# A two-layer attention, scan and convolution block: the attention's value product turned round, exponentials stationary and values moving

## The chip, the core and the metric

The kernel runs on one core of one Trainium2 chip. The metric is the device time of one execution in microseconds (us). The core's engines each run their own queue of instructions in order: the tensor engine (PE in the profile, its weight loads PEld), the vector engine (DVE), the scalar engine (ACT), GpSimd (POOL) and SyncE (SP), which here issues all DMAs. PE multiplies a stationary operand, loaded first, with a moving one, and writes to PSUM; the others bring the result back to SBUF.

## The reference, cut to what matters

Two layers run over 1024 tokens and a prefix of 256 context tokens, with a width of 1024. In each layer one projection feeds three branches: a bidirectional state space scan (12 heads of 64), an attention with 12 query heads of 64 on 4 key and value heads, and a gated convolution. Their outputs are joined and go through an output projection. In the last layer only the 1024 tokens are carried on. The attention is

```python
s = jnp.einsum('bqkrd,bskd->bkrqs', qi, keys, preferred_element_type=F32) * scale
p = jax.nn.softmax(s, axis=-1).astype(vals.dtype)
return jnp.einsum('bkrqs,bskd->bqkrd', p, vals)
...
attn_lat = attend(ql, jnp.concatenate([kl, kc], axis=1), jnp.concatenate([vl, vc], axis=1)) * jax.nn.silu(ga)
```

All of it is in float32. The 1024 queries attend to all 1280 keys, the 256 context queries of the first layer to the 256 context keys alone.

## The kernel before, in words

A layer runs through an input projection (`phase_b`), the attention (`attn_prep`, `attn`) beside the scan (`ssd`), and the output projection (`wout_half`, `out_half`). Projections and scores split each float32 operand into a high and a low part of type F32R, and multiply the parts; the value product, the scan and the column of twos use plain F32.

The attention works on units: a pair of query heads `p` (6 of them) and a group `g` of 256 queries. Layer 0 has 5 groups, the last of them the context, and layer 1 has 4, so there are 30 and 24 units. A unit of ordinary queries goes over 10 key tiles of 128 keys, a context unit over 2. A unit has these parts:

- `prep` (`qprep`, `kprep`): query and key blocks are loaded, split and transposed on PE into the PSUM bank "v", of which there is one, and copied to `q_a`, `q_b`, `k_a`, `k_b`.
- `maxima`: scores with queries on the partitions (rows `m<-k_a,q_a`), whose row maxima DVE takes (`a_sm`, L924). They become a row beside the queries, so that the score matmul subtracts them.
- `scores`: for each key tile, scores with keys on the partitions and 2 x 256 queries along the free axis (rows `m<-q_a,k_a` and `m<-q_b,k_b`), and their exponentials `a_p` by ACT (128x512). DVE and POOL add the exponentials of pairs of key tiles up (L963, L967, L970), which leaves one 128x512 tile `a_a2` a unit.
- `values`: for each key tile two matmuls. The stationary operand is a value block of 128 keys x 64, the moving one the exponentials of one head, 128 keys x 256 queries. The two heads use the two 64-column halves of the array and fill partitions 0 to 63 and 64 to 127 of a bank of PSUM pool "t". The output is feature-major: 128 features of the head pair by 256 queries. A plain F32 matmul shows in the trace as two passes, each with its load.
- `finish`: two matmuls with a stationary block of twos on `a_a2` give twice the sum of the exponentials, spread over all features (rows `t<-a_a,twos`). DVE takes the reciprocal (L994) and multiplies (L995), POOL multiplies by the gate (L996), and a DMA stores the block into `ya_d`. The two stands for a half that the gate in `ga_d` lacks.

The loop at the end of `attn` interleaves the units. In each step of a key tile it calls the scores, the maxima of the unit two ahead, the values two steps behind (VLAG), and at step 7 the finish of a unit whose values are complete. Each call sets a priority (`at`); the framework simulates the engines and fixes the order of each engine's queue from these priorities and from what is ready in its simulation. The scan has priorities of its own in the same stretch of time, and its matmuls (rows `x<-...`) stand in the same PE queue. It uses many POOL operations; `s_e` with `s_xd` also uses the two halves of the array. The output weights are loaded into memory that the scan frees, those of the second half of the output into memory that the attention frees.

In the code below, `mk` takes a tile from a pool, `mm` is a matmul (out, stationary, moving, start, stop; L191), `tr` a transpose on PE (L194), `act` an activation (L197); V, G and Y are DVE, POOL and SP.

Of the kernel before, what the change touches and what calls it, by code (L numbers as in the profile page):

```python
# [11 lines left out]
ALU = mybir.AluOpType  # L12
# [10 lines left out]
SSD_PACE = 25.0  # L23
AT_PACE = 1.2
VLAG = 2
PTB = 5
AHEAD = 2
FLAG = 7
NG = [0, 1]
A2B = 1  # L30
GATP = True
GB = 2
DM = 1024
NLAT = 1024
# [124 lines left out]
def build(tc, a, out, depth=DEPTH, dump=None):  # L159
# [53 lines left out]
                mm(ps, xs(xi, k), ys(yi, k), first and i == 0, last and i == n - 1)  # L213
                i += 1

# [1 line left out]
    ccr = mk(cp, [128, KT, 2], "ccr")  # L217
    Y.dma_start(out=ccr, in_=a["cc"])
    msk = mk(cp, [128, 3, 128], "msk")
# [3 lines left out]
    V.tensor_copy(idr, idf)  # L223
    ones = mk(cp, [128, 128], "ones")
    G.memset(ones, 1.0)
    twos = mk(cp, [128, 64], "twos")
    G.memset(twos, 2.0)
    neg = mk(cp, [128, 16], "neg")
    G.memset(neg, -0.5)
    colc, rowc = [], []  # L230
# [15 lines left out]
    msh = [mk(cp, [128, KT, 2], f"msh{l}") for l in range(depth)]  # L246
    msc = [mk(cp, [128, KT, 2], f"msc{l}") for l in range(depth)]

# [1 line left out]
    x_d = [[dr([128, 512], f"x_d{t}_{n}") for n in range(2)] for t in range(NT)]  # L250
    q_d = [dr([NT, 128, 256], f"q_d{j}") for j in range(3)]
    k_d = dr([NT, 128, 256], "k_d")
# [15 lines left out]
        ts(V, tmp, i, scale, ALU.mult, EPS, ALU.add)  # L268
        G.tensor_tensor(o, tmp, neg[:, :n], ALU.pow)

# [1 line left out]
    def ada(l, j0, nj, lo, w, wp, bufs):  # L272
        ps = mk(pt, [128, 512], "t")
        for k in range(KT):
# [37 lines left out]
    def rc(l, n):  # L312
        return rowc[l][:, RO[n][0]:RO[n][0] + RO[n][1]]

# [1 line left out]
    def norm_tile(l, t, h, wp):  # L316
        r = 0 if t < 8 else 1
        xt = mk(wp, [128, DM], "n_x", bufs=3 if l == 0 else 1)
# [24 lines left out]
        V.tensor_copy(hh[:, :, tok], hf)  # L343
        (V if t % 2 else G).tensor_tensor(hl[:, :, tok], hf, hh[:, :, tok].bitcast(F32), ALU.subtract)

# [1 line left out]
    def wblock(p, rp, src, tag, bufs, e=None, rtag="wr", rbufs=1):  # L347
        shape = list(src.shape)
        hi = mk(p, shape, tag + "h", F32R, bufs=bufs)
# [18 lines left out]
        wk = wblock(wp, np_, a["wtm"][l, 0], "wk", 1, V, "n_h", 2 if l == 0 else 1)  # L368
        return st, h, ws, wk, ns, np_

    # ================= norm =================
    def norms(l, nh, b0, pace):
        for t in range(NT):
            at(b0 + t * pace)
            norm_tile(l, t, nh[1], nh[5])
        nh[4].close()

    # ================= SSD steps, decays and weights =================
    def ssd_prep(l, pp, tp):
        def sm(tag):  # L380
            return mk(pp if tag in ("d_dt", "d_cum", "d_ec", "d_et", "d_wd") else tp, [128, NT, 24], tag)
# [46 lines left out]
        Y.dma_start(out=cum_d.rearrange("(i r) t -> r i t", i=2), in_=ct)  # L428
        return dt, cum, ec, et, wd

    # ================= input projection =================
    def phase_b(l, nh, b0, pp):
        last = l == depth - 1
        st, st_r, s1 = ExitStack(), ExitStack(), ExitStack()
# [6 lines left out]
            norms(l, nh, b0 - 5, 2.6)  # L441
            nst.close()

# [1 line left out]
        qp = pool(s1, f"qp{l}")  # L445
        at(b0)
        rope = mk(qp, [128, 2, NT, 64], "rope")
# [81 lines left out]
                ada_gate(ll, ap_, 2)  # L529
        s1.close()  # L530

# [1 line left out]
        b2 = b0 + 130  # L533
        cmp_ = pool(st, f"cm{l}")
        s2 = ExitStack()
# [108 lines left out]
            block(i)  # L644
        s2.close()

# [1 line left out]
        s3 = ExitStack()  # L648
        tlp = pool(s3, f"tl{l}")
        g0 = b2 + 9 * 26  # L650
# [53 lines left out]
        st.close()  # L704
        return g0 + 8 * 26, sv, st_r

    # ================= SSD =================
    def ssd(l, sp, c0, sv):
        last = l == depth - 1
        at(c0)  # L710
# [123 lines left out]
                state(c, 0, xt, bt, hf, ho)  # L834
                hf = ho

    # ================= attention =================
    def attn_prep(l, kp, c0):
        last = l == depth - 1
        ng = 4 if last else 5  # L840
        at(c0 - 6)
        vs = mk(kp, [128, NT, 256], "vs")
        Y.dma_start(out=vs, in_=v_d.rearrange("t p f -> p t f"))
        kst = {}

        def kprep(v):
            ka = mk(kp, [128, NT, 128], "k_a", F32R, bufs=2)
            kb = mk(kp, [65, NT, 128], "k_b", F32R, bufs=2)
            act(kb[64:65], ones[64:65].unsqueeze(1).to_broadcast([1, NT, 128]), AF.Copy)
            for t0 in (0, 4, 8):  # L850
                n = min(4, NT - t0)
                kt = mk(kp, [128, 4, 64], "k_t", bufs=1)[:, 0:n]
                Y.dma_start(out=kt, in_=k_d[t0:t0 + n, :, 64 * v:64 * v + 64].rearrange("t p f -> p t f"))
                h2 = mk(kp, [128, 4, 2, 64], "k_h", F32R, bufs=1)[:, 0:n]
                l1 = mk(kp, [128, 4, 64], "k_l", F32R, bufs=1)[:, 0:n]
                act(h2, kt.unsqueeze(2).to_broadcast([128, n, 2, 64]), AF.Copy)
                V.tensor_tensor(l1, kt, h2[:, :, 0].bitcast(F32), ALU.subtract)
                ps = mk(pv_, [128, 4, 128], "v", F32R)
                for t in range(n):
                    tr(ps[:, t, :], h2[:, t].rearrange("p a d -> p (a d)"), idr)  # L860
                act(ka[:, t0:t0 + n, :], ps[:, 0:n, :], AF.Copy)
                ps = mk(pv_, [128, 4, 128], "v", F32R)
                for t in range(n):
                    tr(ps[0:64, t, :], l1[:, t], idr)
                act(kb[0:64, t0:t0 + n, :], ps[0:64, 0:n, :], AF.Copy)
            kst[v] = ka, kb

        def qprep(p, g):
            qt = mk(kp, [128, 2, 128], "q_t", bufs=2)
            Y.dma_start(out=qt, in_=q_d[p // 2][2 * g:2 * g + 2, :, 128 * (p % 2):128 * (p % 2) + 128].rearrange("t p f -> p t f"))  # L870
            sg = mk(kp, [128, 2, 2, 2, 64], "q_g", F32R, bufs=2)
            qv = qt.rearrange("p t (x d) -> p x t d", x=2)
            act(sg[:, :, :, 0, :], qv, AF.Copy)
            V.tensor_tensor(sg[:, :, :, 1, :], qv, sg[:, :, :, 0, :].bitcast(F32), ALU.subtract)
            ps = mk(pv_, [128, 2, 2, 128], "v", F32R)
            for x in range(2):
                for t in range(2):
                    tr(ps[:, x, t, :], sg[:, x, t].rearrange("p a d -> p (a d)"), idr)
            qa = mk(kp, [128, 2, 2, 128], "q_a", F32R, bufs=AHEAD + 2)
            qb = mk(kp, [65, 2, 2, 128], "q_b", F32R, bufs=AHEAD + 2)  # L880
            act(qa, ps, AF.Copy)
            act(qb[0:64], ps[0:64], AF.Copy)
            return qa, qb

        qst = {}
        units = [(p, g) for p in range(6) for g in range(ng)]

        def prep(i, t0):
            if i < len(units):
                p, g = units[i]  # L890
                at(t0)
                for v in sorted({(2 * p + y) // 3 for y in range(2)}):
                    if v not in kst:
                        kprep(v)
                qst[i] = qprep(p, g)

        for i in range(AHEAD + 1):
            prep(i, c0 - 5)
        return vs, kst, qst, prep, units

    def attn(l, ap, c0, pre):
# [3 lines left out]
        def key_tiles(i):  # L905
            return range(NT) if units[i][1] < 4 else range(8, NT)
# [1 line left out]
        def kv(i, x):  # L908
            return (2 * units[i][0] + x) // 3

        # row maxima of the scores, as a row beside the queries
        def maxima(i):
            qa, qb = qst[i]
            pcs = [(0, 512), (512, 512), (1024, 256)] if units[i][1] < 4 else [(1024, 256)]
# [15 lines left out]
            act(qb[64:65], ps[64:65].rearrange("p (x t) q -> p x t q", x=2), AF.Copy)  # L930
            yield

        pts, acs = {}, {}

        # exponentials of the scores by key tile, and their sums over the key tiles
        def scores(i):
            qa, qb = qst.pop(i)
            pts[i] = {}
            kt = key_tiles(i)
            ng = NG[i % len(NG)] if len(kt) > 2 else 0  # L940
            ac = [mk(ap, [128, 2, 512], f"a_ac{x}") for x in range(2)] if len(kt) > 2 else None
            prev = []
            same = kv(i, 0) == kv(i, 1)
            for b in kt:
                ps = mk(pm, [128, 512], "m")
                for x in range(1 if same else 2):
                    ka, kb = kst[kv(i, x)]
# [2 lines left out]
                    rb = qb.rearrange("p x t q -> p (x t q)") if same else qb[:, x].rearrange("p t q -> p (t q)")  # L950
                    mm(o, ka[:, b, :], ra, True, False)
                    mm(o, kb[:, b, :], rb, False, True)
                if b % 2 == 0:
                    pt2 = mk(ap, [128, 2, 512], "a_p", bufs=PTB)
                act(pt2[:, b % 2], ps, AF.Exp)
                pts[i][b] = pt2[:, b % 2]
                if b % 2:
                    j = b // 2
                    if not prev or j == ng + 1:
                        prev.append(pt2)  # L960
                    else:
                        e, o = (G, ac[0]) if j <= ng else (V, ac[1])
                        e.tensor_tensor(o, prev[-1], pt2, ALU.add)  # L963
                        prev[-1] = o
                yield
            if len(prev) > 1:
                V.tensor_tensor(ac[1], prev[0], prev[1], ALU.add)  # L967
                prev = [ac[1]]
            a2 = mk(ap, [128, 512], "a_a2", bufs=A2B)
            V.tensor_tensor(a2, prev[0][:, 0], prev[0][:, 1], ALU.add)  # L970
            acs[i] = a2
            yield

        def values(i):
            p, g = units[i]
            kt = key_tiles(i)
            gat = mk(ap, [128, 256], "a_g", bufs=GB)
            Y.dma_start(out=gat, in_=ga_d[p][:, 256 * g:256 * g + 256])  # L978
            ps = mk(pt, [128, 2, 256], "t")
            for b in kt:  # L980
                for y in range(2):
                    mm(ps[64 * y:64 * y + 64, 0, :], vs[:, b, 64 * kv(i, y):64 * kv(i, y) + 64],
                       pts[i][b][:, 256 * y:256 * y + 256], b == kt[0], b == NT - 1)
                yield
            pts.pop(i)
            fin.append((i, ps, gat))

        def finish(i, ps, gat):
            p, g = units[i]
            a2 = acs.pop(i)  # L990
            for y in range(2):
                mm(ps[64 * y:64 * y + 64, 1, :], twos[:, 0:64], a2[:, 256 * y:256 * y + 256], True, True)
            rc_ = mk(ap, [128, 256], "a_rc", bufs=1)
            V.reciprocal(rc_, ps[:, 1])  # L994
            V.tensor_tensor(rc_, ps[:, 0], rc_, ALU.mult)  # L995
            (G if GATP else V).tensor_tensor(gat, gat, rc_, ALU.mult)  # L996
            Y.dma_start(out=ya_d[p][:, 256 * g:256 * g + 256], in_=gat)

        t0 = c0
        for i in range(AHEAD):  # L1000
# [38 lines left out]
            finish(*fin.pop(0))  # L1039
        return t0  # L1040

    # ================= output projection =================
    def wout_half(l, n, wp, t0):
        w = []
        for k in [12, 13, 14, 15] + list(range(12)):
# [138 lines left out]
```

## Time and profile before

| | us |
|---|---|
| median of 3 runs | 2948.47 (2947.58 to 2953.2) |
| span of the profiled execution | 2948.2 |
| PE busy | 2799.6 (95%) |
| PE weight loads busy | 2059.6 (70%) |
| DVE busy | 2156.6 (73%) |
| ACT busy | 1066.1 (36%) |
| POOL busy | 1169.3 (40%) |
| attention, first to last exponentials, layer 0 | 826 to 1380 |
| attention, first to last exponentials, layer 1 | 2271 to 2757 |

A row of the timeline gives the start (us from the span's start), the length, the engine, the source line, the operation, the tiles it writes and reads, the shapes and how many neighbours were merged into it. `128*64` on a PE row are the rows and columns of the array in use. In brackets stands how long the engine was idle before it and what ended that; "issue" means that the profile shows nothing it waited for. A row of a stretch gives start:end and length, and then the busy time of PE, PEld, DVE, ACT and POOL with their instructions, the granted PE clock, the share of DMA and GB/s. A row of a group of instructions gives the count, then busy us and mean ns of one, then the idle time of the engine before them. A row of waits gives the waiting engine and line, what it waited for, total us, times and the longest.

### The profile page before, as it was taken

What the parts mean: (1) busy time and instruction counts of PE and PEld (TensorE: products, weight loads), DVE (VectorE), ACT (ScalarE), POOL (GpSimd) and SP (SyncE); (2) the same over time, 40 slices, a digit from 0 to 9 for tenths busy, and PEclk for the clock granted to TensorE, in tenths of its full rate; (3) what the DMA queues carried; (4) which work ended last, traced back from release to release, by engine and by line L of the source; (5) the groups of instructions that cost most, each with busy time, mean ns of one, the idle gap of its engine ahead of it and who ended that gap; (6) DMA issues with size and microseconds to landing.
All of it is one profiled execution on the core that took longest, in us unless ns stands there. A gap on an engine that the chain in (4) does not pass through costs nothing. (4 is left out here: it accounts for less than half of the span.)

```text
span 2948.2 us, 40643 instructions
## 1 busy us (share of the span) xinstructions
PE 2799.6 (95%) x15492; PEld 2059.6 (70%) x15492; DVE 2156.6 (73%) x2987; ACT 1066.1 (36%) x1801; POOL 1169.3 (40%) x832
## 2 busy tenths in 40 slices
PE   5999998999999999999999999989998999999998
PEld 3888777888745555554777998877786565555676
DVE  4476899973288988977535576999734988998744
ACT  4212221122245555454335322222223455544532
POOL 2244222232156767662112353132322676774111
PEclk8999999999999999999999999999999999999999
DMA  6542111223332323223745322112335222321554
GB/s 235 191 160 77 50 54 65 81 100 105 120 125 82 98 71 100 71 70 104 209 151 158 120 78 73 50 56 99 107 120 168 68 87 85 95 64 47 175 158 141
DMA packets 284035, 314.43 MB, mean 107 GB/s; under 512 B 27606, under 2 KB 219190, under 8 KB 282814
## 3 DMA queue, kind: packets, MB, share of 16 engines
q1 hardware_dynamic: 283838, 311.82, 33.3%
q8 instruction: 122, 2.00, 0.3%
q14 instruction: 75, 0.61, 0.1%
HBM read 236.25 MB, written 75.50 MB: 106 GB/s over the span
## 5 line engine op out<-in xcount | busy, mean ns | idle before, releaser
L191 PE MATMUL m<-hh,wth 128*128 128x512 f32 (+1 forms) x1440 | 533.5, 371 | 0.0
L191 PE MATMUL m<-hl,wth 128*128 128x512 f32 (+1 forms) x1440 | 532.6, 370 | 0.0
L191 PE MATMUL m<-hh,wtl 128*128 128x512 f32 (+1 forms) x1440 | 532.5, 370 | 0.0
L197 ACT ACTIVATE a_p<-m 128x512 f32<-128x512 f32 x492 | 288.8, 595 | 384.9 <-PE m L191 379.0
L357 POOL TENSOR_TENSOR wtl<-wr,wth 128x1024 fp32r<-128x1024 f32 x68 | 215.4, 3168 | 435.3 <-ACT wth L197 435.2
L206 DVE SCALAR_TENSOR_TENSOR cac<-up,cmw,cac 128x1295 f32<-128x1295 f32 (+1 forms) x240 | 383.4, 1619 | 1.8
L924 DVE TENSOR_REDUCE a_sm<-m 128x1 f32<-128x512 f32 (+1 forms) x600 | 331.6, 581 | 42.0 <-PE m L191 39.8
L191 PE MATMUL t<-a_p,vs 128*64 128x256 f32 x1968 | 320.6, 404 | 0.0
L191 PEld LDWEIGHTS m<-hh,wth 128*128 128x128 f32 x1440 | 273.4, 190 | 47.5
L191 PEld LDWEIGHTS m<-hh,wtl 128*128 128x128 f32 x1440 | 273.0, 190 | 47.5
L191 PEld LDWEIGHTS m<-hl,wth 128*128 128x128 f32 x1440 | 273.1, 190 | 47.4
L191 PE MATMUL m<-q_a,k_a 128*128 128x512 f32 (+1 forms) x656 | 261.0, 409 | 5.2 <-DVE a_sm L924 4.5
L191 PE MATMUL m<-k_a,q_a 128*128 128x512 f32 (+1 forms) x600 | 246.2, 436 | 9.0 <-DVE a_sm L924 4.5
L191 PE MATMUL m<-woh,yh 128*128 128x512 f32 x576 | 227.4, 397 | 9.2 <-issue 4.9
L191 PE MATMUL m<-woh,yl 128*128 128x512 f32 x576 | 229.5, 399 | 4.7 <-DVE yl L1076 4.3
L191 PE MATMUL m<-wol,yh 128*128 128x512 f32 x576 | 227.1, 395 | 0.0
L191 PE MATMUL m<-q_b,k_b 65*128 65x512 f32 (+1 forms) x656 | 218.3, 344 | 0.0
L191 PEld LDWEIGHTS m<-q_a,k_a 128*128 128x128 f32 x656 | 125.4, 191 | 110.6 <-issue 52.5
L191 PEld LDWEIGHTS t<-a_p,vs 128*64 128x64 f32 x1968 | 100.8, 135 | 136.4 <-issue 106.3
L197 ACT ACTIVATE wth<-wr 128x1024 fp32r<-128x1024 f32 (+1 forms) x84 | 89.3, 1063 | 268.3 <-DMA wr<-in_wfm 151.8
L191 PEld LDWEIGHTS m<-k_a,q_a 128*128 128x128 f32 x600 | 113.0, 195 | 93.5 <-issue 31.1
L191 PE MATMUL m<-wth,hh 128*128 128x256 f32 (+1 forms) x608 | 173.6, 288 | 1.2 <-ACT wth L197 0.6
(239 smaller groups left out, 5589.7 us busy)
## 6 DMA issues: line engine op xcount, KB each, us to landing
wr<-in_wfm SPq DMA_DIRECT2D x68, 512.0 KB, 3.6
s_cb<-cum_d SPq DMA_DIRECT2D x72, 384.0 KB, 3.5
ada_w<-in_adaw SPq DMA_DIRECT2D x32, 512.0 KB, 3.9
wor<-in_wout SPq DMA_DIRECT2D x64, 256.0 KB, 3.0
s_x<-xt_d SPq DMA_DIRECT2D x38, 384.0 KB, 3.1
yf<-ys_d SPq DMA_DIRECT2D x36, 384.0 KB, 4.1
yf<-ya_d SPq DMA_DIRECT2D x36, 384.0 KB, 4.3
yf<-yc_d SPq DMA_DIRECT2D x36, 256.0 KB, 3.0
```

Source lines behind the costliest of these rows:

```text
L191: P.matmul(o, l, r, start=start, stop=stop)
L197: S.activation(o, i, f, **k)
L206: V.scalar_tensor_tensor(o, i, s, i1, op0, op1)
L357: (e or G).tensor_tensor(lo[:, s], raw, hi[:, s].bitcast(F32), ALU.subtract)
L924: V.tensor_reduce(sm[:, 2 * x + t, j:j + 1], ps[:, 0:kn], axis=AX.X, op=ALU.max)
```

## The change: what it does

The value product swaps its operands. For each key tile there are now four matmuls instead of two, one for each head and each 128 queries. The exponentials (128 keys x 128 queries) are stationary on the full array, and the value block with a column of twos appended (128 keys x 65) moves. The output is token-major: 128 queries by 64 features, and in column 64 twice the sum of the exponentials. So the adds over key tiles on DVE and POOL and the matmuls with the block of twos go away. `finish` takes a reciprocal of four columns and multiplies by it on DVE, transposes two blocks of 128x128 on PE into bank "v" to come back to feature-major, and multiplies by the gate on DVE (it was POOL). The values are loaded by four DMAs, one for each value head, into a tile with 65 columns a head, whose last column is set to two. The exponentials lie in 13 buffers of one key tile instead of 5 of two.

```diff
-PTB = 5
+PTB = 13
...
-NG = [0, 1]
-A2B = 1
-GATP = True
...
-    twos = mk(cp, [128, 64], "twos")
-    G.memset(twos, 2.0)
...
-        vs = mk(kp, [128, NT, 256], "vs")
-        Y.dma_start(out=vs, in_=v_d.rearrange("t p f -> p t f"))
+        vs = mk(kp, [128, NT, 4, 65], "vs")
+        G.memset(vs[:, :, :, 64:65], 2.0)
+        for v in range(4):
+            Y.dma_start(out=vs[:, :, v, 0:64], in_=v_d[:, :, 64 * v:64 * v + 64].rearrange("t p f -> p t f"))
...
-                if b % 2 == 0:
-                    pt2 = mk(ap, [128, 2, 512], "a_p", bufs=PTB)
-                act(pt2[:, b % 2], ps, AF.Exp)
-                pts[i][b] = pt2[:, b % 2]
-                if b % 2:
...
-                        e, o = (G, ac[0]) if j <= ng else (V, ac[1])
-                        e.tensor_tensor(o, prev[-1], pt2, ALU.add)
...
-                V.tensor_tensor(ac[1], prev[0], prev[1], ALU.add)
...
-            V.tensor_tensor(a2, prev[0][:, 0], prev[0][:, 1], ALU.add)
+                e = mk(ap, [128, 512], "a_p", bufs=PTB)
+                act(e, ps, AF.Exp)
+                pts[i][b] = e
...
-            ps = mk(pt, [128, 2, 256], "t")
+            ps = mk(pt, [128, 4, 128], "t")
             for b in kt:
-                for y in range(2):
-                    mm(ps[64 * y:64 * y + 64, 0, :], vs[:, b, 64 * kv(i, y):64 * kv(i, y) + 64],
-                       pts[i][b][:, 256 * y:256 * y + 256], b == kt[0], b == NT - 1)
+                for x in range(2):
+                    for t in range(2):
+                        j = 2 * x + t
+                        mm(ps[:, j, 0:65], pts[i][b][:, 128 * j:128 * j + 128], vs[:, b, kv(i, x), :],
+                           b == kt[0] and j == 0, b == NT - 1 and j == 3)
...
-            a2 = acs.pop(i)
-            for y in range(2):
-                mm(ps[64 * y:64 * y + 64, 1, :], twos[:, 0:64], a2[:, 256 * y:256 * y + 256], True, True)
-            rc_ = mk(ap, [128, 256], "a_rc", bufs=1)
-            V.reciprocal(rc_, ps[:, 1])
-            V.tensor_tensor(rc_, ps[:, 0], rc_, ALU.mult)
-            (G if GATP else V).tensor_tensor(gat, gat, rc_, ALU.mult)
+            rc_ = mk(ap, [128, 4], "a_rc", bufs=2)
+            V.reciprocal(rc_, ps[:, :, 64])
+            o = mk(ap, [128, 2, 2, 64], "a_o", bufs=2)
+            V.tensor_tensor(o.rearrange("p t x d -> p x t d"),
+                            ps[:, :, 0:64].rearrange("p (x t) d -> p x t d", x=2),
+                            rc_.rearrange("p (x t) -> p x t", x=2).unsqueeze(3).to_broadcast([128, 2, 2, 64]), ALU.mult)
+            ps2 = mk(pv_, [128, 4, 128], "v")
+            for t in range(2):
+                tr(ps2[:, t, :], o[:, t].rearrange("p x d -> p (x d)"), idf)
+            V.tensor_tensor(gat, ps2[:, 0:2, :], gat, ALU.mult)
```

More of the change, by code (lines that the diff above doesn't have):

```diff
@@ L931, in maxima @@
             yield
-        pts, acs = {}, {}
+        pts = {}
         def scores(i):
@@ L938, in scores @@
             pts[i] = {}
[L939 to L942, printed above, removed]
             same = kv(i, 0) == kv(i, 1)
-            for b in kt:
+            for b in key_tiles(i):
                 ps = mk(pm, [128, 512], "m")
@@ L952, in scores @@
                     mm(o, kb[:, b, :], rb, False, True)
-                if b % 2 == 0:
-                    pt2 = mk(ap, [128, 2, 512], "a_p", bufs=PTB)
-                act(pt2[:, b % 2], ps, AF.Exp)
-                pts[i][b] = pt2[:, b % 2]
-                if b % 2:
[L958 to L961, printed above, removed]
-                        e, o = (G, ac[0]) if j <= ng else (V, ac[1])
-                        e.tensor_tensor(o, prev[-1], pt2, ALU.add)
-                        prev[-1] = o
-                yield
[L966 to L972, printed above, removed]
+                e = mk(ap, [128, 512], "a_p", bufs=PTB)
+                act(e, ps, AF.Exp)
+                pts[i][b] = e
+                yield
         def values(i):
@@ L976, in values @@
             kt = key_tiles(i)
-            gat = mk(ap, [128, 256], "a_g", bufs=GB)
-            Y.dma_start(out=gat, in_=ga_d[p][:, 256 * g:256 * g + 256])
-            ps = mk(pt, [128, 2, 256], "t")
+            gat = mk(ap, [128, 2, 128], "a_g", bufs=GB)
+            Y.dma_start(out=gat, in_=ga_d[p][:, 256 * g:256 * g + 256].rearrange("p (t q) -> p t q", t=2))
+            ps = mk(pt, [128, 4, 128], "t")
             for b in kt:
-                for y in range(2):
-                    mm(ps[64 * y:64 * y + 64, 0, :], vs[:, b, 64 * kv(i, y):64 * kv(i, y) + 64],
-                       pts[i][b][:, 256 * y:256 * y + 256], b == kt[0], b == NT - 1)
+                for x in range(2):
[3 more added lines that the diff above has]
+                           b == kt[0] and j == 0, b == NT - 1 and j == 3)
                 yield
@@ L989, in finish @@
             p, g = units[i]
-            a2 = acs.pop(i)
-            for y in range(2):
-                mm(ps[64 * y:64 * y + 64, 1, :], twos[:, 0:64], a2[:, 256 * y:256 * y + 256], True, True)
-            rc_ = mk(ap, [128, 256], "a_rc", bufs=1)
[L994 to L997, printed above, removed]
+            rc_ = mk(ap, [128, 4], "a_rc", bufs=2)
[8 more added lines that the diff above has]
+            V.tensor_tensor(gat, ps2[:, 0:2, :], gat, ALU.mult)
+            Y.dma_start(out=ya_d[p][:, 256 * g:256 * g + 256].rearrange("p (t q) -> p t q", t=2), in_=gat)
         t0 = c0
```

## The prediction

> **What bounds the kernel now.** I read the page's list of engines first, then the stretches of the two attention stages, then the timeline of the tensor engine inside one of them, and last the waits of that engine.
>
> ```profile
> span 2948.2 us, 40643 instructions
> PE 2799.6 (95%) x15492; PEld 2059.6 (70%) x15492; DVE 2156.6 (73%) x2987; ACT 1066.1 (36%) x1801; POOL 1169.3 (40%) x832
> ...
> 826.00:1380.00 554.00, 537.75 (x3157) 306.54 (x3156) 466.42 (x662) 278.87 (x476) 346.13 (x212) 0.98 0.27 81
> 1380.00:1410.00 30.00, 24.13 (x96) 17.97 (x97) 18.88 (x24) 11.02 (x17) 1.47 (x2) 0.89 0.63 190
> ...
> 2271.00:2757.00 486.00, 476.17 (x2842) 270.85 (x2841) 423.83 (x597) 250.62 (x430) 303.05 (x179) 1.00 0.26 81
> ```
>
> The first exponentials of layer 0 run at 826, the last ones at 1380; in layer 1 it is 2271 and 2757. The change acts in these 1040 us. PE is busy for 97% of them and DVE for 86% (466.42 + 423.83), so the two look like rivals for the bound. Busy PE counts modelled ends, so the row does not decide it; the timeline does. Here is one key tile's value product between score matmuls, first PE, then the weight loads (PEld):
>
> ```profile
> 1094.80 0.40 PE L191 MATMUL m<-q_b,k_b 65*128 65x512 f32 x1
> 1095.13 0.65 PE L191 MATMUL t<-a_p,vs 128*64 128x256 f32 x4
> 1095.71 0.50 PE L191 MATMUL m<-k_a,q_a 128*128 128x512 f32 x1
> 1096.05 0.40 PE L191 MATMUL m<-q_a,k_a 128*128 128x512 f32 x1
> 1096.28 0.40 PE L191 MATMUL m<-q_b,k_b 65*128 65x512 f32 x1
> ...
> 1095.13 0.20 PEld L191 LDWEIGHTS t<-a_p,vs 128*64 128x64 f32 x4 [0.37 <-issue]
> 1095.71 0.19 PEld L191 LDWEIGHTS m<-k_a,q_a 128*128 128x128 f32 x1 [0.39 <-issue]
> 1095.82 0.19 PEld L191 LDWEIGHTS m<-q_a,k_a 128*128 128x128 f32 x1
> ```
>
> A 512-column score matmul takes 0.23 us to the start of the next (1096.05 to 1096.28). From 1094.80 to 1096.05 are 1.25 us; two such matmuls (1094.80, 1095.71) take 0.46, so the four value rows cost **0.79 us**. Loads normally start while the matmul before them runs (1095.82). At the change from the full array (128*128) to its two 64-column halves (128*64), and again at the way back, the load has no releaser and a gap of 0.37 and 0.39: it starts only when the array is empty, and then its own time is exposed too. So the tensor engine is not waiting for DVE there; it pays for the change of shape.
>
> ```profile
> L191 PEld LDWEIGHTS t<-a_p,vs 128*64 128x64 f32 x1968 | 100.8, 135 | 136.4 <-issue 106.3 <-ACT a_p L197 4.4 <-ACT q_b L197 1.5
> ...
> L191 PE MATMUL t<-a_a,twos 128*64 128x256 f32 x216 | 35.1, 396 | 4.9 <-DVE a_a L970 4.8
> ...
> L197 ACT ACTIVATE a_p<-m 128x512 f32<-128x512 f32 x492 | 288.8, 595 | 384.9 <-PE m L191 379.0 <-DVE a_sm L924 1.8 <-DVE a_ac L963 0.9
> ```
>
> There are 492 key tiles (a_p rows) and 1968 value loads, each with its matmul row: two matmuls a tile, each shown as two passes. 136.4 us of idle before those loads, at 0.36 each, is some 379 bursts: most tiles pay the change alone. ACT stands 379 us in front of a_p waiting for PE, so PE sets the pace of attention. The waits of PE itself from 826 to 1400, longest first, agree:
>
> ```profile
> PE m L191 <- DVE a_sm L924: 4.7, 6, 1.6
> PE t L191 <- DVE a_a L970: 4.5, 4, 2.5
> ...
> PEld m L191 <- DVE a_sm L924: 21.1, 45, 2.0
> PEld t L191 <- DVE a_a L970: 6.1, 6, 2.8
> ```
>
> **The change part by part.** *Value product.* Now 492 x 0.79 = 389 us. Some tiles follow one another without a change between (cheaper), some have a single full matmul between two bursts (its load is exposed twice); I let these cancel. Bounds: all alone 389, and 379 alone with the other 113 at the bare 0.44 (below) 349.
>
> After it, each tile has four matmuls with a 128-column f32 stationary operand and 65 moving columns, so 8 passes, 3936 in all, on the full array. No row has this shape. The nearest are 128-column f32 loads with a matmul of one column, and with one of 128 columns:
>
> ```profile
> 1062.93 0.30 PEld L191 LDWEIGHTS x<-ones,s_s 128*128 128x128 f32 x2 [0.39 <-DVE a_rc L994]
> 1063.15 0.19 PEld L191 LDWEIGHTS m<-q_a,k_a 128*128 128x128 f32 x1
> 1063.26 0.19 PEld L191 LDWEIGHTS m<-q_b,k_b 65*128 65x128 f32 x1
> ...
> 1025.28 0.71 PE L191 MATMUL x<-s_cT,s_bT 128*128 128x128 f32 x4
> 1025.74 0.36 PE L191 MATMUL m<-k_a,q_a 128*128 128x256 f32 x1
> ...
> 1025.28 0.52 PEld L191 LDWEIGHTS x<-s_cT,s_bT 128*128 128x128 f32 x4 [0.39 <-issue]
> 1025.72 0.19 PEld L191 LDWEIGHTS m<-k_a,q_a 128*128 128x128 f32 x1
> ```
>
> Loads start 0.11 us apart in both (two from 1062.93 to 1063.15, the next at 1063.26; four from 1025.28 to 1025.72): once matmuls are short, the load alone sets the step. 65 columns lie between 1 and 128, so 0.11 is bounded from both sides, and it is set by the 128 stationary columns, which the change does not shrink. 3936 x 0.11 = **433 us** (0.107 to 0.112: 421 to 441). If nothing of a matmul hid behind a load, a pass would be 0.11 + 65/256 x 0.22 = 0.166, which is the far end. The same rows show f32 and the m matmuls next to each other with a load that starts early (1025.72), so a change of type costs nothing and I drop the gaps of 0.37 and 0.39 with the half arrays.
>
> [...]
>
> *Column of twos.* 216 rows are 54 units of four. Behind a value burst a unit costs little, alone it costs a burst:
>
> ```profile
> 1010.01 0.65 PE L191 MATMUL t<-a_p,vs 128*64 128x256 f32 x4
> 1010.50 0.60 PE L191 MATMUL t<-a_a,twos 128*64 128x256 f32 x4
> 1011.03 0.39 PE L191 MATMUL m<-k_a,q_a 128*128 128x256 f32 x1
> ```
>
> From first row to the next full matmul 1.02 us, against 0.58 without the twos (1095.13 to 1095.71): 0.44, or two passes of 0.22. Bounds 54 x 0.44 = 24 and 54 x 0.79 = 43; I take 32.
>
> *Transposes.* Two a unit, 108, at the same 0.11 of a 128-column load: 12 us.
>
> So PE's own work goes from 389 + 32 = 421 to 433 + 12 = 445: **+24 us**.
>
> *DVE and POOL.* These go, or shrink:
>
> ```profile
> L963 DVE TENSOR_TENSOR a_ac<-a_ac,a_p 128x1024 f32<-128x1024 f32 x72 | 119.7, 1663 | 10.8 <-ACT a_p L197 10.2
> ...
> L994 DVE RECIPROCAL a_rc<-t 128x256 f32<-128x256 f32 x54 | 94.4, 1749 | 9.7 <-PE t L191 7.7 <-POOL a_g L996 1.8
> ...
> L963 DVE TENSOR_TENSOR a_ac<-a_p,a_p 128x1024 f32<-128x1024 f32 x48 | 75.3, 1568 | 6.0 <-ACT a_p L197 5.9
> ...
> L970 DVE TENSOR_TENSOR a_a<-a_ac 128x512 f32<-128x512 f32 x48 | 50.5, 1053 | 0.2
> ...
> L967 DVE TENSOR_TENSOR a_ac<-a_p,a_ac 128x1024 f32<-128x1024 f32 x24 | 37.9, 1579 | 0.0
> ...
> L967 DVE TENSOR_TENSOR a_ac<-a_ac,a_ac 128x1024 f32<-128x1024 f32 x24 | 37.2, 1550 | 1.1 <-DVE a_ac L963 0.5
> ...
> L995 DVE TENSOR_TENSOR a_rc<-t,a_rc 128x256 f32<-128x256 f32 x54 | 22.2, 412 | 0.1
> ...
> L963 POOL TENSOR_TENSOR a_ac<-a_p,a_p 128x1024 f32<-128x1024 f32 x24 | 59.8, 2491 | 45.8 <-ACT a_p L197 45.7
> ...
> L996 POOL TENSOR_TENSOR a_g<-a_g,a_rc 128x256 f32<-128x256 f32 x54 | 47.9, 888 | 85.8 <-DVE a_rc L995 65.9 <-issue 10.2 <-DMA yf<-ya_d 6.9
> ```
>
> DVE loses the sums (119.7 + 75.3 + 50.5 + 37.9 + 37.2 = 321) and nearly all of the reciprocal's 94.4 (4 columns for 256), and gains the gate product, 54 x 0.41 as in L995 = 22: about 390 of 2157. POOL loses 108. That hides behind PE, so its worth is only the waits that DVE puts on PE. In layer 0 these are 21.1 + 6.1; less the 0.36 that is the array's own in each of the 45 + 6 gaps, 9. Layer 1 is alike, so 18 to 54 in all; as the longest are over 2 us and other DVE operations end gaps too, I take **-25**.
>
> *Moved and added waits.* The two transposes now stand in PE's queue behind reciprocal and product of DVE; behind them wait the next unit's scores, and ACT for those. DVE is then free for half of the stage (890 - 390 of 1040 busy), and the unit ended several key tiles earlier, so 0; uncovered it would be about 0.6 a unit, 32. They also take the one "v" bank, held for one 0.41 product. The gate's load and store stay. The value load is four DMAs of 256-byte runs instead of one:
>
> ```profile
> L843 SPq DMA_DIRECT2D vs<-v_d x2: 370/370/371, 766.5 to 2214.3; - x2
> ```
>
> They are issued 60 and 57 us before the first exponentials and add three issues of 0.37 to SP's queue, ahead of the key and query loads: 0, and 1.1 a layer if those were waited for.
>
> *Tail.* From 1380 to 1410 PE has 24.13 of 30 us, while output weights arrive after the scan has freed its memory. POOL's 65.9 us in front of a_g, with scan work queued behind it, go, so the scan ends sooner: **-10** (0 to -15). In layer 1 the second half's weight loads start at the end of attention whatever happens: 0.
>
> Sum: 24 - 25 - 10 = -11 on a profiled span of 2948.2. The median of the runs is 2948.47, 0.3 above it: **2937**.
>
> **Rivals.** *Waits stay* (they are PE's own or ACT's, and the transposes add some): +24, 15 us of waits gone and nothing gained at the tail give 2957 (2950 to 2965). For it: only 9 us in layer 0 are surely DVE's. Against it: DVE loses a quarter of its stage.
>
> *DVE was the bound* after all (86% busy): all 54 us of its waits and the whole tail go, 24 - 54 - 15 = -45: 2903. Against it: the gaps in the timeline have no releaser.
>
> *A pass takes longer than a load*: the 65 columns do not hide fully, 0.135 as the middle between 0.11 and 0.166. 3936 x 0.025 = +98: 3035. It decides from 0.113 a pass on, where the 11 us are used up. Against it: the s_cT rows.
>
> *The gaps are not the half array's* but come with every value burst, whatever its shape: 379 x 0.36 = +136, 3073. Against it: full-array f32 neighbours have none. [...]
>
> [...]
>
> **How the numbers follow.** Forecast 0.45; waits stay 0.24; DVE the bound 0.14; longer passes 0.10; gaps stay 0.05; one after the other 0.02. The forecast's own range is 2920 to 2950. The last two lie beyond the range; half of "longer passes" and half of the lowest case are left out as well: 2903 to 2985. 0.2% (6 us) is about what a measurement tells from no change. Faster: 0.35 of the forecast and 0.14, 0.49. Within 0.2%: 0.09 of the forecast and 0.13 of "waits stay", 0.22. Slower: the rest, 0.29.
>
> **What would show it.** Right: rows t<-vs,a_p, 128*128, 128x65, x3936, with loads 0.11 apart and none with a gap of 0.37 before the first; PE rows 15492 + 1968 - 216 + 108 = 17352; DVE near 1766 and POOL near 1061 busy; each attention stage within 10 us of 554 and 486. Wrong: loads of a_p more than 0.113 apart; gaps without a releaser still around the bursts; PE waiting for DVE a_o in front of the transposes; the scan's last store coming after the last exponentials.

## The result and the profile after

The changed kernel took 3008 us (median of four executions, 2976 to 3082) beside 2951 for the kernel before, where 2937 was forecast and 2985 was the upper end of the range. The ratio is 1.0100 (95% interval 1.0065 to 1.0134). That interval rests on the two executions with the higher mean clock (2976 and 2983); the other two (3034, which is the profiled one, and 3082) ran at a lower one, 0.956 and 0.939 for 0.973 and 0.971, and that clock turns out to be the larger part of the answer. Run again later it took 3020 (2980 to 3023), ratio 1.0199 (1.0133 to 1.0265).

The page of the changed kernel: span, busy time of the engines, the granted clock in 40 slices, and the groups of the value product.

```profile
span 3031.8 us, 44130 instructions
...
PE 2898.6 (96%) x17352; PEld 2466.5 (81%) x17352; DVE 1807.3 (60%) x2819; ACT 1068.1 (35%) x1801; POOL 1000.1 (33%) x755
...
PEclk7999999999999999999999999999999999985799
...
L188 PEld LDWEIGHTS t<-vs,a_p 128*128 128x128 f32 x3936 | 558.4, 205 | 40.1 <-issue 0.3
L188 PE MATMUL t<-vs,a_p 128*128 128x65 f32 x3936 | 546.3, 280 | 0.0
```

The change does what it says: 17352 PE rows and 3936 value passes on the full array; DVE and POOL lost 349 and 169 us. The idle time in front of the value loads fell from 136.4 to 40.1 us, and what had no releaser from 106.3 to 0.3. New is the dip (8 5 7) at the end of the row of clock digits. The stretches of the attention, first to last exponentials; layer 1 is cut where the dip begins, and its first row starts 10 us before the exponentials do. The third number from the end is the granted clock:

```profile
831.00:1394.00 563.00, 552.77 (x4079) 482.47 (x4080) 296.16 (x592) 286.62 (x490) 261.53 (x172) 0.98 0.29 87
...
2271.00:2710.00 439.00, 433.69 (x3246) 379.22 (x3245) 242.87 (x474) 219.94 (x373) 225.49 (x149) 1.00 0.28 85
2710.00:2839.00 129.00, 128.84 (x510) 118.48 (x511) 35.05 (x67) 39.42 (x69) 0.00 (x0) 0.50 0.15 47
```

For 129 us PE is busy without a break and is granted **half the clock**. It starts 510 passes there; at the rate of the row above (3246 in 439, 7.4 a us) they would take 69, so 60 us are lost. The exponentials of layer 1 run from 2281 to 2839. In the kernel before, the last exponentials of layer 0 start at 1377.6, so its stage ends at 1378 and not at the 1380 given above. So the 83.6 us between the two spans divide so: start of layer 0 +5, its attention 563 for 552 +11, between the stages (1394 to 2281 for 1378 to 2271) -6, attention of layer 1 558 for 486 +72, of which 60 are the clock's, and the end +2.

POOL has nothing left in the stretch at half clock: the scan is over. Its last store, by the store's group (first and last start, in us):

```profile
L820 SPq DMA_DIRECT2D ys_d<-s_yo x18: 370/384/1265, 906.8 to 2695.8; - x18
```

It is issued at 2696, and the clock falls at 2710. Just before it falls, PE stands idle:

```profile
2707.07 0.78 PE L188 MATMUL t<-vs,a_p 128*128 128x65 f32 x6
2707.78 1.36 ACT L194 ACTIVATE yh<-yf 128x768 fp32r<-128x768 f32 x2 [3.76 <-DMA ox<-x_d]
2710.16 0.69 PE L191 MATMUL v<-msk,a_o 128*128 128x128 f32 x2 [2.31 <-ACT q_b L194]
```

```profile
2706.80:2710.20 3.40, 1.09 (x11) 0.95 (x9) 1.54 (x3) 2.42 (x5) 0.00 (x0) 0.96 0.86 302
```

ACT waits 3.76 us for a DMA of the output projection, and PE waits 2.31 behind it, in front of the transposes, for ACT to copy `q_b` out of the one bank "v". In the 3.40 us before the fall PE is busy for 1.09. So the fall begins after a gap, and it then lasts while PE is busy without a break (128.84 of 129 us). It ends at 2843, where 512-column matmuls of the output projection stand among the value passes.

The weight loads of two key tiles before the fall, and of six passes after it:

```profile
1042.36 0.98 PEld L188 LDWEIGHTS t<-vs,a_p 128*128 128x128 f32 x8
1043.26 0.53 PEld L188 LDWEIGHTS x<-s_cT,s_bT 128*128 128x128 f32 x4
...
2764.94 1.40 PEld L188 LDWEIGHTS t<-vs,a_p 128*128 128x128 f32 x6
2766.22 0.33 PEld L188 LDWEIGHTS m<-q_a,k_a 128*128 128x128 f32 x1
```

Eight loads take 0.90, **0.1125 a pass**; at half clock six take 1.28, 0.213. So a load slows down with the granted clock, 0.50 there.

### The profile page after: what moved, and what is told of

Read it like the earlier page. It is cut to its first block, busy times and chain, and to the rows that moved or that the text cites. A ratio compares the mean times of both kernels' runs of the same rounds, so it can differ in the third digit from the quotient of the medians.

```text
span 3031.8 us, 44130 instructions
## 1 busy us (share of the span) xinstructions
PE 2898.6 (96%) x17352; PEld 2466.5 (81%) x17352; DVE 1807.3 (60%) x2819; ACT 1068.1 (35%) x1801; POOL 1000.1 (33%) x755
## 5 line engine op out<-in xcount | busy, mean ns | idle before, releaser
L188 PEld LDWEIGHTS t<-vs,a_p 128*128 128x128 f32 x3936 | 558.4, 205 | 40.1 <-issue 0.3
L188 PE MATMUL t<-vs,a_p 128*128 128x65 f32 x3936 | 546.3, 280 | 0.0
L921 DVE TENSOR_REDUCE a_sm<-m 128x1 f32<-128x512 f32 (+1 forms) x600 | 341.6, 590 | 183.4 <-PE m L188 179.5
L188 PE MATMUL m<-q_a,k_a 128*128 128x512 f32 (+1 forms) x656 | 268.2, 419 | 0.9 <-ACT a_p L194 0.7
L188 PE MATMUL m<-q_b,k_b 65*128 65x512 f32 (+1 forms) x656 | 232.0, 364 | 0.0
L188 PE MATMUL m<-wtl,hh 128*128 128x256 f32 (+1 forms) x608 | 173.0, 285 | 0.6 <-DVE wtl L352 0.6
L188 PE MATMUL m<-wth,hl 128*128 128x256 f32 (+1 forms) x608 | 173.6, 286 | 0.0
```

Source lines behind the costliest of these rows:

```text
L188: P.matmul(o, l, r, start=start, stop=stop)
L921: V.tensor_reduce(sm[:, 2 * x + t, j:j + 1], ps[:, 0:kn], axis=AX.X, op=ALU.max)
```

## The experiments

Three questions: does the clock stay down because the multiplications are short; what do the orientation and the relief of DVE cost and bring each at full clock; and would another way have kept the relief.

### More and fewer moving columns

The value pass keeps its 128-column load and its count; the moving columns change, and with them in part the order of PE's queue, which the framework fixes from simulated durations. Row by row, 17256 of the 17352 PE rows stand where they stood with 65 columns in the version with 96, 15485 in that with 128 and 15801 in that with 33. 128 and 96 columns take further values along, whose results nobody reads:

```diff
-                        mm(ps[:, j, 0:65], pts[i][b][:, 128 * j:128 * j + 128], vs[:, b, kv(i, x), :],
+                        c = 260 * b + 65 * kv(i, x)
+                        mm(ps[:, j, 0:128], pts[i][b][:, 128 * j:128 * j + 128], vs[:, c:c + 128],
```

> The changed kernel with 128 moving columns instead of 65 in every value matmul: the 63 extra columns run into the neighbouring values, and what they give is not read. Theory (the clock): in the changed kernel a value pass loads for 0.112 us and multiplies for 65/256 x 0.22 = 0.056, and the granted clock falls to half where such passes make up the stream; with 128 columns a pass multiplies for 0.11, inside the load, so its step stays 0.112, the granted clock of the second attention stage goes from 0.55 in its last 137 us to 0.98 or more, and the time is 2950 to 2970, every execution within 0.5% of the others. Rival (the work): the time comes from the loads or from new waits and the clock only goes with it; then 2976 to 3080 as before, or more, since the matmuls are longer.

> The changed kernel with 96 moving columns, between 65 (clock falls to half for 133 us) and 128 (it does not). By the clock theory the share of a step that multiplies goes from 0.5 to 0.75 of it: few or no long stretches at half, 2953 to 2985, and less scatter than with 65. If the width of 128 had helped in another way than by time spent multiplying (a full bank row, say), it would stay at 2976 or more.

33 columns leave half of each head's values out and use the other half twice:

```diff
-                        mm(ps[:, j, 0:65], pts[i][b][:, 128 * j:128 * j + 128], vs[:, b, kv(i, x), :],
+                        mm(ps[:, j, 0:33], pts[i][b][:, 128 * j:128 * j + 128], vs[:, b, kv(i, x), 32:65],
```

> The changed kernel with 33 moving columns (32 value columns and the twos) instead of 65: half of each head's values is left out of the product, and finish uses the other half twice. Theory (the clock): the step stays 0.112, set by the load, but a pass multiplies for only 0.03 us of it, so the clock is granted at half for longer than in the changed kernel: mean clock below 0.956, time 3050 to 3250. Rival (the work): the loads are the same and the matmuls shorter, so 2976 to 3035, not above the changed kernel.

And the changed kernel as it is, measured together with the 96 columns on one chip (33 and 128 columns were together on another):

> The changed kernel once more, unaltered, beside the other two: if the clock's fall is a matter of a threshold that the value passes stand close to, its executions scatter by more than 1% (2976 to 3082 so far) and the granted clock goes with the time; if not, they agree to 0.5%.

| moving columns | median us (range) | ratio to before (95%) | mean clock of the profile |
|---|---|---|---|
| 33 | 3094 (3087 to 3098) | 1.0492 (1.0461 to 1.0522) | 0.933 |
| 65, again | 3020 (2980 to 3023) | 1.0199 (1.0133 to 1.0265) | 0.972 |
| 96 | 2961 (2955 to 2972) | 1.0037 (1.0018 to 1.0056) | 0.980 |
| 128 | 2956 (2951 to 2959) | 1.0021 (1.0007 to 1.0035) | 0.982 |

Twice the work in every value pass makes the kernel **53 us faster** than 65 columns (2956 for 3008), and half of it makes it 86 us slower. The clock digits and the attention stages with 128 columns:

```profile
PEclk8999999999999999999999999999999999999999
```

```profile
829.00:1379.00 550.00, 544.42 (x4083) 477.39 (x4083) 289.94 (x593) 287.80 (x490) 261.36 (x172) 0.99 0.30 89
...
2256.00:2762.00 506.00, 498.65 (x3737) 440.53 (x3737) 266.49 (x524) 254.81 (x438) 220.31 (x146) 1.00 0.28 82
```

No long fall is left. With 33 columns there are two, one behind each scan (whose last stores are at 1294 and 2750):

```profile
PEclk8999999999999999955999999999999999985799
```

```profile
1308.00:1458.00 150.00, 149.28 (x595) 136.15 (x595) 44.65 (x96) 44.40 (x77) 0.00 (x0) 0.50 0.15 44
...
2762.00:2905.00 143.00, 142.19 (x566) 131.19 (x567) 39.29 (x78) 44.27 (x77) 0.00 (x0) 0.50 0.14 43
```

Both start 13 to 14 us after the last store, much as the one with 65 columns did. Before the first one stands no such gap; the stretch before it has PE busy for 11.75 of 12 us at full clock:

```profile
1296.00:1308.00 12.00, 11.75 (x99) 11.21 (x97) 6.38 (x16) 7.02 (x13) 0.55 (x1) 1.00 0.69 211
```

In the repeated run, in its profiled execution of 2980, the fall is short:

```profile
2272.00:2787.00 515.00, 511.78 (x3736) 454.26 (x3737) 267.71 (x523) 254.78 (x437) 219.72 (x145) 0.97 0.27 81
2703.00:2737.00 34.00, 34.00 (x144) 31.68 (x143) 16.79 (x32) 14.11 (x26) 0.00 (x0) 0.50 0.31 96
```

With 96 columns the clock falls at the same place and after a like gap, but comes back within 7 us; the rows are PE's gap, the fall and what follows it:

```profile
2694.26 0.39 PE L188 MATMUL m<-q_a,k_a 128*128 128x256 f32 x1 [2.21 <-ACT a_p L194]
...
2696.00:2703.00 7.00, 7.00 (x32) 6.70 (x31) 5.16 (x10) 3.74 (x8) 0.00 (x0) 0.51 0.41 119
2703.00:2769.00 66.00, 65.67 (x482) 60.62 (x482) 27.74 (x56) 34.78 (x62) 0.00 (x0) 1.00 0.27 78
```

In layer 0 of the changed kernel the clock is at half for some 14 us:

```profile
1324.00:1337.50 13.50, 12.36 (x41) 9.89 (x42) 10.28 (x19) 6.79 (x12) 0.00 (x0) 0.50 0.36 117
```

So with 65 columns the executions differ: in layer 1 the clock stays down for 34 us in one and 133 in another, and the time scatters from 2976 to 3082. What the profiled executions show is that the clock stays down for long with 33 columns (150 and 143 us) and with 65 (133 and 34) and not with 96 (7 us) and 128, while loads and rows stay the same, and with 96 columns nearly the whole order of the queue. What decides it is not shown, nor why the same kernel differs so from one execution to the next. An estimate for such a pass, from the 0.44 us of the twos in the kernel before (two passes of 256 columns on each half), is that the multiplication fills 0.056 of its 0.1125 us; with 128 columns it would be 0.11. The three longest falls (129, 143 and 150 us) come where these passes are no longer mixed with the scan's: they begin some 13 to 14 us after its last store.

### The orientation and DVE's relief, each by itself

First the kernel before without the additions of the exponentials; the twos take a constant tile. Then the changed kernel with 128 columns (so at full clock), with the additions done as before into tiles that nobody reads (and the exponentials in five buffers of two tiles again).

```diff
-                        e, o = (G, ac[0]) if j <= ng else (V, ac[1])
-                        e.tensor_tensor(o, prev[-1], pt2, ALU.add)
...
-            V.tensor_tensor(a2, prev[0][:, 0], prev[0][:, 1], ALU.add)
-            acs[i] = a2
+            acs[i] = flat
```

> The kernel before with the sums of the exponentials left out: VectorE's and GpSimd's additions (321 and 60 us busy) are gone, and the product with the twos takes a constant tile, so that every result is divided by a constant. This prices the relief of VectorE by itself, with the tensor engine's work the same. By the forecast's term (waits on VectorE worth 25 us, bounds 18 to 54): 2896 to 2932, about 2925. If the waits are PE's own (the rival 'waits stay'): 2935 to 2952. VectorE busy about 1840, PE's idle in front of m on a_sm L924 below 10 us in each stage if it was VectorE's load that made it.

> The changed kernel with 128 moving columns, and VectorE and GpSimd do the additions of the exponentials as before, into tiles that nobody reads (the exponentials are kept in pairs, five pairs deep, as before). VectorE busy about 2120, GpSimd 1060. This is the other side of the same price, with the clock at full. Relief of VectorE worth 25: 2981. Worth nothing once the value product no longer stops the array: 2952 to 2962. If VectorE's load was what held the stage: above 2990.

Measured 2912.1 (ratio 0.9877, 0.9858 to 0.9896) and 2989.9 (1.0148, 1.0124 to 1.0172). With the runs above this is a square of four:

| ratio to before | with the additions | without them | without by with |
|---|---|---|---|
| values stationary, half arrays | 1 (before) | 0.9877 | 0.9877 |
| exponentials stationary, 128 columns | 1.0148 | 1.0021 | 0.9875 |
| second by first | 1.0148 | 1.0146 | |

The two effects add within these intervals (128 columns come from another chip, each ratio is to the kernel before on its own): **leaving out the additions is worth 36 us and the new orientation costs 43**, whatever the other does. Without the additions DVE is busy for 310 us less and POOL for 133, and the two were not taken apart; the smaller reciprocal, which also relieves DVE, counts to the orientation here. The stages say the same. The kernel before without the additions, then the changed one with them (DVE is the third busy time):

```profile
827.00:1355.00 528.00, 518.79 (x3144) 300.94 (x3143) 313.39 (x558) 282.85 (x482) 281.60 (x200) 1.00 0.30 90
2240.00:2719.00 479.00, 475.99 (x2829) 271.40 (x2828) 288.21 (x499) 254.65 (x436) 236.16 (x168) 1.00 0.29 86
```

```profile
827.00:1400.00 573.00, 554.21 (x4079) 482.83 (x4079) 435.52 (x704) 288.58 (x490) 320.46 (x185) 0.98 0.28 85
2280.00:2792.00 512.00, 500.43 (x3725) 442.74 (x3726) 405.77 (x629) 255.95 (x436) 281.27 (x157) 0.99 0.27 81
```

Both stages together: before 1038, without additions 1007; 128 columns 1056, with additions 1085. The orientation costs 47 to 49 there, and 8 to 13 come back between the stages (from the last exponentials of layer 0 to the first of layer 1: 893 and 885 with values stationary, 880 and 877 with exponentials stationary). PE's busy time without additions rises from 994.78 to 1043.07, by 48.

### The old orientation on the full array

Stationary [values | 64 columns of twos], moving all exponentials: no half arrays, no additions, no transposes.

```diff
+            vs[v] = mk(kp, [128, NT, 128], "vs", bufs=2)
+            G.memset(vs[v][:, :, 64:128], 2.0)
...
+                if kv(i, 0) == kv(i, 1):
+                    mm(ps.rearrange("p y q -> p (y q)"), vs[kv(i, 0)][:, b], pts[i][b], b == kt[0], b == NT - 1)
```

> The value product in the old orientation, but on the full array: the stationary operand is 64 value columns and 64 columns of two, exponentials move (512 or 2 x 256 columns). Sums come with the product, as in the change; no transposes, one reciprocal of 512 columns on DVE, gate on POOL. If the gaps of 0.37 and 0.39 are the price of going to half arrays and back, they vanish: 492 x 4 x 0.22 = 433 us against 421 for product and twos before, less 25 of waits on DVE, and full-length matmuls keep the clock at 0.97 or more: 2925 to 2960. If the gaps belong to any value burst, 136 us more: 3070 to 3100.

Measured 2965.9, ratio 1.0061 (1.0041 to 1.0082), above the 2925 to 2960 expected. PE's rows show why the full array gains nothing for the tensor engine:

```profile
1101.87 1.02 PE L188 MATMUL t<-a_p,vs 128*128 128x512 f32 x2
1102.32 0.68 PE L188 MATMUL m<-k_a,q_a 128*128 128x256 f32 x1
1102.84 1.02 PE L188 MATMUL t<-a_p,vs 128*128 128x512 f32 x2
1103.30 0.79 PE L188 MATMUL m<-q_a,k_a 128*128 128x512 f32 x1
1103.93 0.40 PE L188 MATMUL m<-q_b,k_b 65*128 65x512 f32 x1
```

From 1102.84 to 1103.93 are 1.09 us; less 0.23 for the score matmul a key tile costs 0.86, more than the 0.79 of the half arrays with their change of shape. A key tile is two plain float32 passes of 512 columns here, so one takes 0.43; four passes of 256 on the halves had a bare cost of 0.44 in all, where at this rate they would take 0.86 one after the other. So the two halves had worked **at the same time**, and the full array gives that up. Why the missing additions, worth 36 us above, bring nothing here is not shown; DVE is relieved by less, as its reciprocal now has 64x512 elements and takes 181 us for 94.

### Value rows in runs of five key tiles

The kernel before, but the value rows of five key tiles wait for the exponentials of the last, so that the array changes its shape less often (VLAG goes from 2 to 1 with it).

```diff
+RUN = 5
...
+                e = min(kt[-1], b + RUN - 1 - (b - kt[0]) % RUN)
...
+                    if b < e:
+                        dep(ins, exs[i, e])
-                yield
+                if b == e:
+                    yield
```

> The kernel before with its value products held back until five key tiles are ready, so that they run one behind another: about 100 bursts instead of some 490, nothing else changed. If each burst pays about 0.36 us for the change to half arrays and back and PE sets the pace, 390 x 0.36 = 140 us go, as far as DVE (890 busy of the 1040 us) lets them: 2810 to 2870. If DVE or a chain through it set the pace, 2940 to 2960.

Measured 2950.7, ratio 1.0003 (0.9985 to 1.0020): no gain, as expected if DVE or a chain through it set the pace, where PE as the bound would have given 80 us and more. PE's busy time fell from 2799.6 to 2728.5, but it now waits. The two stages, and the waits of the weight loads in layer 0 (total us, times, longest):

```profile
824.00:1367.00 543.00, 492.11 (x3135) 328.44 (x3136) 465.15 (x657) 272.77 (x471) 350.70 (x213) 0.95 0.25 77
2268.00:2748.00 480.00, 441.56 (x2823) 294.28 (x2824) 427.52 (x592) 245.61 (x424) 301.80 (x178) 0.97 0.26 80
```

```profile
PEld t L192 <- DVE a_a L975: 25.9, 14, 6.6
PEld m L192 <- DVE a_sm L929: 25.4, 42, 2.1
```

Before, the twos waited 6.1 us for DVE's sums in this layer, and the score matmuls 21.1. The clock is lower too, 0.95 and 0.97 for 0.98 and 1.00 before; from these an estimate is that the half clock takes up to 16 and 14 us (0.03 of each stage). With the additions left out as well:

> Values in runs of five key tiles, and the sums left out as in b_nosum: both the array's changes of shape and VectorE's load go at once. If the gain of the runs (PE busy 71 us less, time the same) was eaten by VectorE, the two together give 2950 - 80 to 140: 2810 to 2870. If it is the scan's chain or ScalarE's exponentials that come next, as the run with the additions on PE (2942) hints: 2900 to 2940. If the clock is granted at half for longer when the cover is gone: PEclk digits below 9 in the attention stages and a time above 2940.

2859.4, ratio 0.9695 (0.9668 to 0.9721): 53 us below the same without runs. Alone the runs bring nothing, alone the relief brings 36, and together they bring 87. The groups of this run:

```profile
L202 ACT ACTIVATE a_p<-m 128x512 f32<-128x512 f32 x492 | 282.9, 595 | 254.3 <-PE m L192 250.9
...
L192 PEld LDWEIGHTS t<-a_p,vs 128*64 128x64 f32 x1968 | 136.9, 138 | 96.0 <-ACT a_p L202 21.5 <-issue 11.7 <-ACT q_b L202 1.5
```

The idle time without a releaser fell from 106.3 to 11.7 us, and ACT stands 254 us before a_p instead of 385. So the tensor engine and the additions, most of them DVE's, bound the kernel before **together**: what PE saves at the changes of shape it then loses to waits for DVE and to the lower clock in the same stages (0.95 and 0.97), until DVE has less to do. How much of the loss is the clock's was not measured.

### Versions that give the result

Runs of five, and a split of the additions between the engines. In the first the twos add all four partial sums on PE; the second gives POOL one more addition in every second unit; the third, with POOL's addition kept, lets DVE join the two partial sums again and leaves only the last, two halves, to the twos.

```diff
-            V.tensor_tensor(a2, prev[0][:, 0], prev[0][:, 1], ALU.add)
-            acs[i] = a2
+                    acs[i] = [t_[:, x] for t_ in prev for x in range(2)]
...
-NG = [0, 1]
+NG = [1, 1]
```

> The kernel before with value products in runs of five key tiles, and with DVE's last two additions of a unit (L967, L970) left to PE: the matmul with the block of twos takes four partial sums instead of one, in the same run of half-array matmuls. PE saves about 390 x 0.36 = 140 us of array changes and gets 48 x 3 x 0.44 = 63 back; DVE loses 37.9 + 37.2 + 50.5 = 126 of its 890. If PE and DVE were both near the bound in the kernel before, so that relieving only one of them brought nothing, relieving both brings 40 to 90: 2860 to 2910. If something else holds the stage, the chain of the scan or ACT, it stays at 2940 to 2955.

> The version with value rows in runs of five key tiles and the last additions done by the twos on the tensor engine (2942 so far), with one more pair addition in every second unit given from VectorE to GpSimd: 24 x 1.6 = 38 us less on VectorE, 24 x 2.5 = 60 us more on GpSimd. If VectorE's load is still what eats the gain of the runs (leaving its sums out altogether was worth 86 us there): 2920 to 2938. If GpSimd's additions come late for the twos, or it is the scan that waits for GpSimd: 2942 to 2960.

> As the kernel beside it, but VectorE joins the two partial sums again (48 additions of about 1.6 us, 75 us) and the twos take only the two halves, so the tensor engine has 48 x 0.86 = 41 us less of sums. VectorE near 2080, PE near 2750. If VectorE's load counts more: 5 to 20 us above the other; if PE's does: 5 to 20 us below it.

Measured 2942.4 (0.9965, 0.9950 to 0.9980), 2951.0 (1.0008, 0.9995 to 1.0020) and **2916.8 (0.9892, 0.9868 to 0.9917)**. The first two missed the gain hoped for (2860 to 2910 and 2920 to 2938) and landed where something else than DVE was expected to hold the stage; the sums on PE had given most of its saving back (PE busy 2774.8 and 2788.5, for 2799.6 before and 2728.5 with the runs alone). The third beats both kernels, and lies 34 us below the second, where 5 to 20 were expected if PE's work counts more. The second has DVE busy 89 us less than the third (2004.2), but PE 53 us more (2788.5), and is the slower: in this pair PE's work counts for more than DVE's. The third, engines and stages:

```profile
PE 2735.6 (94%) x15708; PEld 2118.8 (73%) x15708; DVE 2093.1 (72%) x2909; ACT 1060.6 (36%) x1801; POOL 1215.8 (42%) x856
```

```profile
827.00:1354.00 527.00, 492.24 (x3243) 332.88 (x3245) 426.22 (x620) 274.51 (x476) 372.91 (x224) 0.98 0.28 85
2240.00:2724.00 484.00, 452.25 (x2916) 300.99 (x2915) 396.84 (x560) 246.97 (x429) 321.55 (x191) 0.98 0.27 81
```

PE and DVE are each 64 us below the kernel before. It is 32 us faster, where the same runs of five with DVE's work left as it was brought nothing. POOL, with 47 us more, pays for part of that.

## Why the prediction was wrong

**The step that failed is the price of a value pass, 3936 x 0.11: it holds at full clock only, and the sum put the clock at nothing.** Every duration was taken at the clock of the kernel before, which held 0.98 and 1.00 in its attention stages, and it was never asked whether the new passes keep it. At half clock a pass costs 0.213. With the clock held (128 columns) the change costs 6 us, inside the whole range of 2903 to 2985 though above the forecast's own 2920 to 2950; at 65 columns some 20 (2976) to 126 us (3082) come on top, 53 at the median. The prediction did name that the load alone sets the step; that the array then multiplies half of the time (by the estimate above 0.056 of 0.1125 us) could be worked out from its rows, and no rival drew the consequence.

A second term at nothing, *moved and added waits*, has a part in it: in the profiled execution the fall begins behind a wait of 2.31 us in front of the transposes, for the bank "v". With 96 columns a gap of 2.21 stands at the same place, in front of scores, and the clock is back after 7 us; so the gap alone does not cost the 60.

The granted clock is 0.50 in each stretch shown of 34 us and more. Just before the fall in the changed kernel PE was busy for 1.09 of 3.40 us, but in the fall itself it is busy for 128.84 of 129; and with 33 columns the clock falls where PE had been busy for 11.75 of 12 us. What starts a fall and what sets its length is not shown.

Term by term, with the clock held:

- *Value product, twos and transposes, +24 in PE's work*: 47 to 49 in the stages. **Undersized by half.** The step is 0.1125 where 0.11 was taken, which is 10 us on 3936 passes and at the upper end of the bounds given (0.107 to 0.112). The other 13 to 15 could not be put down to one row.
- *Waits on DVE, -25*: the additions alone are worth 36, by two pairs, POOL's share of them included. Right in kind, inside its bounds (18 to 54), too small. The rival "waits stay" falls with it.
- *Tail, -10*: 8 to 13 between the stages. Right, and the scan does end sooner: its last store of layer 0 is issued at 1294 for 1360. In the profiled execution of the changed kernel it was 6.
- *Twos*: they are in the 47 to 49, and were not measured alone.
- Added up: the orientation with its tail +43, the relief -36, that is +7 for a measured +6, where the forecast had 24 - 10 = +14 and -25, that is -11.

The rivals: *the gaps are not the half array's* is wrong, the gaps without a releaser are gone (106.3 to 0.3 us). That a load starts there only when the array is empty was the author's reading of the rows; the runs show the gap (0.37 and 0.39) and that it goes with the half arrays. *One after the other*, the far end of 0.166 a pass, is wrong: no run shows such a pass at full clock. With 128 columns, where by the estimate above the multiplication (0.11) is about as long as the load (0.1125), attention runs 3737 PE rows in 506 us, 7.4 a us as with 65 columns (3246 in 439), so the two do overlap at full height. *A pass takes longer than a load* gave 3035, close to what the profiled execution took, but for another reason: at full clock the pass is 0.1125, at half clock 0.213, and the load itself is what slows. Its row would be loads 0.135 apart throughout, and there is none. *DVE was the bound* was half right: its additions shared the bound with PE, which no case of the prediction had.

What it would have shown: the row counts came out as said (3936 and 17352); DVE 1807 for 1766 and POOL 1000 for 1061 only roughly; layer 0 was within 10 us of 554 (563), layer 1 not (558 for 486). No wait of the transposes on DVE stands among PE's longest; the one of 2.31 us in front of them is on ACT.

## What to carry to other kernels

A value pass of 65 moving columns cost its weight load here, 0.1125 us, and where such passes ran without the scan's the granted clock stayed at 0.50 for 129 us; the same passes with 128 columns kept it (0.99 and 1.00 in the attention stages), and the kernel was 53 us faster. So where short passes run alone, compare with a version that multiplies more columns than it needs. Before a busy share is read as "not the bound", take that engine's work away on a copy of the kernel: here the vector engine at 86% of its stage shared the bound with the tensor engine, and fewer changes of the array's shape brought nothing by themselves and 53 us once the additions were left out. Matmuls on the two halves of the array ran together here (four passes of 256 columns in 0.44 us), so a change of shape (0.35 us a burst, 0.79 less 0.44) can be worth its price.

## What was unexpected of the hardware

- The tensor engine's clock stays at half (0.50) although the engine is busy all the time: 34 to 150 us in a stretch, and the three longest begin some 13 to 14 us after the scan's last store. With 65 columns a gap of about 2 us stands before it; with 33 it also begins without one. With 96 columns the fall behind such a gap (2.21 us) lasts 7 us, and with 128 no long one was seen (0.99 and 1.00 in the attention stages).
- A weight load runs on the granted clock too: 0.1125 a pass at full, 0.213 at half.
- At 65 columns the same kernel scatters by 3.5% (2976 to 3082), at 96 and 128 by 0.6% and 0.3%.
